# The first load ahead of SyncE's register set-up in an im2col kernel

## Chip, cores, metric

One core of one Trainium2 chip. The metric is the device time of one execution in microseconds (us). All runs used for a verdict are of state "fast". Ratios are the mean time of one kernel's fast runs over that of the other's of the same rounds, so they are not quite the ratio of the medians quoted beside them.

## The reference

```python
# x: (16, 64, 32, 32) float32, kernel_size 3
for b in range(batch):
    col_idx = 0
    for i in range(h_out):              # 30
        for j in range(w_out):          # 30
            patch = x[b, :, i:i + 3, j:j + 3]
            cols[b, :, col_idx] = patch.ravel()
            col_idx += 1                # cols: (16, 576, 900)
```

4.19 MB are read and 33.18 MB are written.

## The kernel before

The partitions carry 8 planes of 32 x 32 each. Two loads bring them in (planes 0 and 1, then the other six), VectorE and ScalarE copy nine shifted windows of each plane, and four stores of two planes each write the result. When the program is otherwise complete, the first load is taken out of the body and put into the program's head, ahead of the barrier of all engines.

```python
    first = load(0, 2 * H)
    load(2 * H, CPP * H)
    # ... (cut)
    for c in range(0, CPP, 2):
        out_tile = out_pool.tile([P, 2, KK, HO, WO], x.dtype, name="out_tile")
        # ... six copies a plane pair on VectorE, three on ScalarE (cut)
        nc.sync.dma_start(
            out=out_v[:, c : c + 2].rearrange("p c n -> p (c n)"),
            in_=out_tile.rearrange("p c kk i j -> p (c kk i j)"),
        )
    return first
# ... (cut)
    tc.compile()
    blocks = tc.nc.main_func.blocks
    load = first.ins
    home = next(b for b in blocks if any(i.name == load.name for i in b.instructions))
    home.instructions = [i for i in home.instructions if i.name != load.name]
    head = list(blocks[0].instructions)
    at = next(
        k
        for k, i in enumerate(head)
        if i.engine == load.engine and type(i).__name__ == "InstDrain"
    )
    head.insert(at, load)
    blocks[0].instructions = head
```

## Time and profile before

| | before |
|---|---|
| time, 3 runs at first | 91.21 us (91.16 to 91.29) |
| span of the profile | 89.6 us |
| DMA queue, share of 16 engines' span | 97.2% |
| first load: issue, first packet, landed | 0.00, 1.01, 4.91 us |
| second load: issue, landed | 0.79, 12.19 us |
| last store landed | 88.81 us |

The span runs from the first instruction of the program to the last. What lies outside of it (1.8 us in the profiled execution) the profile doesn't show. The landing times are those at which a transfer's semaphore reaches its full count. The lines themselves are in the prediction.

### The profile page before, as it was taken

What the parts mean: (1) busy time and instruction counts of PE and PEld (TensorE: products, weight loads), DVE (VectorE), ACT (ScalarE), POOL (GpSimd) and SP (SyncE); (2) the same over time, 40 slices, a digit from 0 to 9 for tenths busy, and PEclk for the clock granted to TensorE, in tenths of its full rate; (3) what the DMA queues carried; (4) which work ended last, traced back from release to release, by engine and by line L of the source; (5) the groups of instructions that cost most, each with busy time, mean ns of one, the idle gap of its engine ahead of it and who ended that gap; (6) DMA issues with size and microseconds to landing.
All of it is one profiled execution on the core that took longest, in us unless ns stands there. A gap on an engine that the chain in (4) does not pass through costs nothing.

```text
span 89.6 us, 96 instructions
## 1 busy us (share of the span) xinstructions
DVE 22.6 (25%) x24; ACT 23.8 (27%) x13; POOL 0.2 (0%) x4
## 2 busy tenths in 40 slices
DVE  0079759900000099500000399100000000000000
ACT  5079759900000099500000399100000000000000
POOL 0000000000000000000000000000000000000000
DMA  5989899999999999947999999999999982999990
GB/s 128 505 384 494 362 463 463 463 463 463 463 463 463 463 463 463 434 174 318 463 463 463 463 463 463 463 463 463 463 463 463 463 347 116 463 463 463 463 463 0
DMA packets 864, 37.37 MB, mean 417 GB/s; under 512 B 96, under 2 KB 96, under 8 KB 96
## 3 DMA queue, kind: packets, MB, share of 16 engines
q1 hardware_dynamic: 864, 37.37, 97.2%
HBM read 4.19 MB, written 33.18 MB: 417 GB/s over the span
## 4 chain that ended last, share of the span: by engine, by line
DMA 49%; DVE 12%; DVEq 1%; issue 0%; SPq 0%
DMA out_dram<-out_tile 36%; DMA in_tile<-in_x_dram 13%; DVE out_tile L57 8%; DVE out_tile L61 2%; DVE out_tile L65 1%; DVEq L89 1%; DVEq L57 0%; SPq L71 0%
## 5 line engine op out<-in xcount | busy, mean ns | idle before, releaser
L55 ACT COPY out_tile<-in_tile 128x2700 f32<-128x2700 f32 x8 | 19.2, 2443 | 31.7 <-DMA out_dram<-out_tile 27.1
L57 DVE COPY out_tile<-in_tile 128x1800 f32<-128x1800 f32 x16 | 16.8, 1092 | 33.7 <-DMA out_dram<-out_tile 27.1
L61 DVE COPY out_tile<-in_tile 128x1800 f32<-128x1800 f32 x4 | 4.4, 1090 | 0.0
L68 ACT COPY out_tile<-in_tile 128x900 f32<-128x900 f32 x4 | 3.8, 938 | 0.0
L65 DVE COPY out_tile<-in_tile 128x900 f32<-128x900 f32 x4 | 2.5, 620 | 0.0
L55 ACT ACT_TABLE_LOAD x1 | 1.3, 1283 | 0.8 <-PEq L118 0.8
L118 POOL MEMSET const-bfloat16-1.0<- 128x1 bf16 x1 | 0.1, 101 | 0.0
L118 POOL MEMSET const-uint8-127<- 128x1 uint8 x1 | 0.1, 101 | 0.0
L118 POOL MEMSET const-float32-0.0<- 128x1 f32 x1 | 0.1, 98 | 0.2 <-issue 0.2
L118 POOL MEMSET const-float32-1.0<- 128x1 f32 x1 | 0.1, 98 | 0.0
## 6 DMA issues: line engine op xcount, KB each, us to landing
out_dram<-out_tile SPq DMA_DIRECT2D x4, 8100.0 KB, 32.4
in_tile<-in_x_dram SPq DMA_DIRECT2D x1, 3072.0 KB, 11.4
in_tile<-in_x_dram SPq DMA_DIRECT2D x1, 1024.0 KB, 4.9
```

The source lines that it names most:

```text
L55: nc.scalar.copy(out=o[:, K : 2 * K], in_=planes(c + s, 1, 0, K, 1))
L57: nc.vector.tensor_copy(out=o[:, ki * K : ki * K + 2], in_=planes(c + s, ki, 0, 2, 1))
L61: nc.vector.tensor_copy(out=o[:, 2:KK:6], in_=planes(c + s, 0, 2, 2, 2 * W))
L65: nc.vector.tensor_copy(out=o[:, 2], in_=in_tile[:, c + s, 0:HO, 2 : 2 + WO])
L68: nc.scalar.copy(out=o[:, 8], in_=in_tile[:, c + s, 2 : 2 + HO, 2 : 2 + WO])
L89: tc.compile()
L118: nc = _bacc.Bacc("TRN2", target_bir_lowering=False, num_devices=1)
```

## The change

Its intent: the six set-up instructions of SyncE (five register moves and one load of a base address) stand ahead of the first load. Putting the load ahead of them should start the transfers earlier.

```diff
     head = list(blocks[0].instructions)
-    at = next(
-        k
-        for k, i in enumerate(head)
-        if i.engine == load.engine and type(i).__name__ == "InstDrain"
-    )
+    at = next(k for k, i in enumerate(head) if i.engine == load.engine)
     head.insert(at, load)
```

## The prediction

> **What bounds the kernel now.** I read the page first (utilisation, the forty slices, the queues), then the chain that ended last, then the instructions of the first microsecond, then the packets one by one.
>
> ```profile
> span 89.6 us, 96 instructions
> DVE 22.6 (25%) x24; ACT 23.8 (27%) x13; POOL 0.2 (0%) x4
> DMA  5989899999999999947999999999999982999990
> q1 hardware_dynamic: 864, 37.37, 97.2%
> ```
>
> The compute engines are busy a quarter of the span. The one DMA queue is busy 97.2% of 16 engines' span: 0.972 x 89.6 = 87.1 us per DMA engine. The transfers are the bound. (The dips in the DMA row are packets of 2.4 us counted in the slice where they begin, not pauses: where I sampled the packets every 0.5 us, all 16 engines had one in flight from 1.5 to 88.0 us but for one moment, near 11.5 us.)
>
> ```profile
> 0.79 11.40 DMA in_tile<-in_x_dram
> 17.95 32.59 DMA out_dram<-out_tile
> 50.56 0.05 DVEq L57
> 55.77 0.54 DVE out_tile L65
> ```
>
> The chain of waits (start, length, what) follows the last *compute* instruction, which is not what ends the program: it stops at 56.3 us, while the last store lands at 88.81 us. So I set the end from packets instead. The first data packet of the first load starts at 1.01 us, the last packet of the last store ends at 88.33 us, 87.32 us in all. One engine carries 8 packets of the first load (mean 378 ns, 3.02 us), 8 of the second (912 ns, 7.30 us) and 32 of the stores (2397 ns, 76.72 us): 87.04 us. A mean engine has 0.28 us without a packet, nearly all of it between the second load's last packet (ends 11.24 to 11.83) and the first store's first (starts 11.54 to 11.84). The engine that ends last has none there: its load ends at 11.834 and its store starts at 11.836. The end is therefore the first packet's start plus uninterrupted transfer.
>
> ```profile
> start us, us, engine line op out<-in xcount [idle before <-releaser]
> 0.00 1.12 SPq L35 DMA_DIRECT2D in_tile<-in_x_dram  x2
> 0.23 0.10 POOL L118 MEMSET const-float32-0.0<- 128x1 f32 x1 [0.23 <-issue]
> 0.78 1.28 ACT L55 ACT_TABLE_LOAD   x1 [0.78 <-PEq L118]
> ```
>
> The timeline of the first microsecond: time zero of the span *is* the first load's issue. It is already ahead of the barrier of all engines. What stands before it on SyncE, five register moves and one load of a base address, is not among the 96 instructions shown; the page leaves register instructions out. The second load is issued at 0.79, right behind the barrier.
>
> ```profile
> L118 SPq DRAIN  x1: 132/132/132, 0.4 to 0.4; - x1
> L118 SPq EVENT_SEMAPHORE  x1: 17/17/17, 0.7 to 0.7; - x1
> L118 POOLq DRAIN  x1: 179/179/179, 0.3 to 0.3; - x1
> L35 SPq DMA_DIRECT2D in_tile<-in_x_dram x2: 332/357/382, 0.0 to 0.8; - x2
> DMA to landing us min/median/max: 4.9/8.2/11.4
> ```
>
> The instructions of the barrier's line and the loads' line (ns min/median/max, first and last start). SyncE's drain (0.43 to 0.56) is the last of the four arrivals; GpSimd's own drain ended at 0.48. So SyncE holds the barrier by about 0.1 us.
>
> [...]
>
> **The change part by part.** *Removed from ahead of the first load:* the set-up, call its time d. No row holds it, so I estimate it from the neighbours. GpSimd has four such moves between the end of its semaphore instruction (158 ns) and its first memset (231 ns): 73 / 4 = at most 18 ns each. SyncE's own short instructions take 7 (drain) to 17 ns (semaphore). So five moves are 5 x 10 to 18 = 50 to 90 ns[...]. Sum d = 70 to 140 ns, middle 100.[...]
>
> *Moved behind the load:* the same d, now between the first issue and SyncE's drain. In absolute time the drain cannot begin later than before, since the same instructions run in another order. It may end earlier: the 132 ns for which it lasts look like waiting for the issue to finish (SyncE's later drains take 7 ns), and now the moves lie in that time. If so the barrier opens up to 564 - 479 = 85 ns earlier and the second load goes up to that much earlier. That is worth nothing: its first packet starts at 3.97 us, and issued at 0.79 it could have started near 0.79 + 0.85 = 1.64 us. There are 2.3 us of slack.
>
> *Added:* nothing. Work, bytes, packets and later waits are the same.
>
> *On the path:* the first packet starts d earlier; the sixteen engines then run through both loads without a pause, so the second load also ends d earlier. The first store needs the copies of the first two planes: landing 4.91 -> copies to 10.6 -> issue 10.69 -> packets 11.54. This branch begins with the first load's landing too, so it also moves by d, and no new gap opens at 11.5. Every store follows, and the end moves by d. Sum: 91.21 - 0.10 = 91.11 us.
>
> **Where I chose.** The measured time must see d. The profiled execution took 91.39 us by the same clock that gave 91.21, against a span of 89.60: 1.79 us lie outside the span[...]. I take it to open before SyncE's set-up[...]; 85% likely. The profile's *span*, which begins at the load itself, will then not show the gain: it stays 89.6.
>
> **The rivals.**
> 1. *No gain at all.* Either the first transfer's start hangs on something tied to the launch and not to the issue, or the measured window opens at the first load. For: the first load needs 1.01 us to its first packet, 0.16 more than a store, and its first packets are slow (up to 1147 ns where the fastest take 309). Against: 35 ns of it is just the longer issue (382 against 347)[...]. Time: 91.2.
> 2. *An early issue is a colder one.* The load would be the first instruction that SyncE fetches, with registers still unset; its issue of 382 ns is already the longest of the six (332 to 347 for the others).[...] Even if it gave back d and 0.1 more: 91.3. Against: [...]nothing in the trace says that the issue waits.
> [...]
> 4. *The barrier takes the gain back*, because SyncE comes later to it. For: SyncE is the last to arrive. Against: only relative to the load, not absolutely, as shown, and the second load has 2.3 us of slack. Time: as predicted, 91.1.
>
> **Range and chances.** The middle is 91.11. Repeats of one kernel spread by 0.13 us (91.16 to 91.29). From below: d at its bound of 0.25 less scatter, 90.95. From above: no gain plus scatter, 91.26. Two per cent would be 1.8 us, more than everything that precedes the first packet (1.01 us) together with the set-up; the change has no part that could reach it. Faster by over 2%: 1%; within 2%: 98%; slower: 1%[...].
>
> **What would show it.** In the changed profile: span 89.6 within 0.15; the first load's issue still at 0.00; everything on the other engines later by d *relative to it*: GpSimd's first memset at 0.33 instead of 0.23, ScalarE's table load at 0.79 to 0.88. SyncE's first drain shorter than 132 ns. The first load lands at 4.9 and the last store at 88.8 after the first issue, as now, and the queue is busy 97%. Wrong would be: the memset still at 0.23 (then d is nil or the load didn't move); a first issue well above 382 ns or a first packet later than 1.1 us (rival 2); a landing later than 5.0 us with the memset moved by d (rival 1); a new hole in the transfers near 11.5 us; or a time under 90.9 or over 91.3.

The sum came to d = 70 to 140 ns, middle 100, and so to 91.21 - 0.10 = 91.11 us. It had two terms: 50 to 90 ns for the five moves, an estimate from the 73 ns and the 7 to 17 ns that stand there, and one for the base-address load, which was the author's assumption. The 0.25 us bound at the range's lower end was not shown. The 0.85 us used for the slack is measured: the first store of `before` is issued at 10.69 us and its first packet starts at 11.54.

## The result and the profile after

The changed kernel took 91.31 us (91.21 to 91.42, 6 runs) against 91.20 us (91.12 to 91.29, 6 runs) for the kernel before; ratio 1.0011, 95% interval 0.9998 to 1.0024. The forecast was 91.11, with a range of 90.95 to 91.26; 91.31 lies outside it.

First the page of the changed kernel:

```profile
span 89.6 us, 96 instructions
q1 hardware_dynamic: 864, 37.37, 97.2%
```

Then its timeline of the first microseconds (start us, us, engine, line, operation):

```profile
0.00 1.12 SPq L35 DMA_DIRECT2D in_tile<-in_x_dram  x2
0.23 0.10 POOL L114 MEMSET const-float32-0.0<- 128x1 f32 x1 [0.23 <-issue]
0.79 1.28 ACT L55 ACT_TABLE_LOAD   x1 [0.79 <-PEq L114]
```

The prediction named this as the test: GpSimd's first memset had to move from 0.23 to 0.33, since the load was to start earlier than everything else. It stayed at 0.23. The prediction also said what that would mean: "d is nil or the load didn't move". Next, all instructions of the barrier's line (now L114, engine, operation, count, ns min/median/max, first and last start in us), and the loads' line:

```profile
L114 POOLq EVENT_SEMAPHORE  x2: 17/17/17, 0.6 to 0.7; - x2
L114 DVEq DRAIN  x1: 10/10/10, 0.1 to 0.1; - x1
L114 ACTq DRAIN  x1: 8/8/8, 0.1 to 0.1; - x1
L114 POOLq INC_SWDGE_SEM  x1: 27/27/27, 0.1 to 0.1; - x1
...
L114 SPq DRAIN  x1: 132/132/132, 0.4 to 0.4; - x1
L114 SPq EVENT_SEMAPHORE  x1: 17/17/17, 0.7 to 0.7; - x1
```

```profile
L35 SPq DMA_DIRECT2D in_tile<-in_x_dram x2: 333/358/383, 0.0 to 0.8; - x2
DMA to landing us min/median/max: 4.9/8.1/11.4
```

In the trace's own numbers the starts of the first 0.9 us are those of before to within 2 ns: SyncE's drain at 432 after 431, the second load's issue at 792 after 791. Had six instructions moved from ahead of the load to behind it, the drain would have come later after the load by their time; behind eight moves that really run it starts at 0.9 us (`moves_behind_scratch`).

**What the program holds.** So I compared the list that the kernel's Python edits with what the traces list. SyncE's head is, in the list and in the trace (starts in ns):

```
edited list, before   move, base load, move x4, LOAD 1, drain, semaphore, branch
edited list, after    LOAD 1, move, base load, move x4, drain, semaphore, branch
trace, before         LOAD 1 at 0, drain at 431, semaphore, LOAD 2 at 791
trace, after          LOAD 1 at 0, drain at 432, semaphore, LOAD 2 at 792
```

The two traces list the same 96 instructions, engine by engine in the same order, and no register move on any engine. I also built both kernels and compared the finished programs, and found the instruction streams equal; that is my own comparison and not a run. What takes the set-up out between the edited list and the chip, no trace shows. By the traces the change is a change of the text alone, and 91.31 against 91.20 must be scatter. The experiments test that, and then the other steps of the prediction in programs in which the set-up is real.

### The profile page after: what moved, and what is told of

It is laid out like the page before. It is cut to its first block, busy times and chain, and to the rows that moved or that the text cites. A ratio compares the mean times of both kernels' runs of the same rounds, so it can differ in the third digit from the quotient of the medians.

```text
span 89.6 us, 96 instructions
## 1 busy us (share of the span) xinstructions
DVE 22.6 (25%) x24; ACT 23.8 (27%) x13; POOL 0.2 (0%) x4
## 3 DMA queue, kind: packets, MB, share of 16 engines
q1 hardware_dynamic: 864, 37.37, 97.2%
## 4 chain that ended last, share of the span: by engine, by line
DMA 49%; DVE 12%; DVEq 1%; issue 0%; SPq 0%
DMA out_dram<-out_tile 36%; DMA in_tile<-in_x_dram 13%; DVE out_tile L57 8%; DVE out_tile L61 2%; DVE out_tile L65 1%; DVEq L89 1%; DVEq L57 0%; SPq L71 0%
## 5 line engine op out<-in xcount | busy, mean ns | idle before, releaser
L114 POOL MEMSET const-uint8-127<- 128x1 uint8 x1 | 0.1, 102 | 0.0
L114 POOL MEMSET const-bfloat16-1.0<- 128x1 bf16 x1 | 0.1, 101 | 0.0
L114 POOL MEMSET const-float32-0.0<- 128x1 f32 x1 | 0.1, 98 | 0.2 <-issue 0.2
L114 POOL MEMSET const-float32-1.0<- 128x1 f32 x1 | 0.1, 98 | 0.0
## 6 DMA issues: line engine op xcount, KB each, us to landing
in_tile<-in_x_dram SPq DMA_DIRECT2D x1, 3072.0 KB, 11.4
```

What stands on the lines that cost most here:

```text
L114: nc = _bacc.Bacc("TRN2", target_bir_lowering=False, num_devices=1)
```

## The experiments

Theory: the set-up isn't in the finished program, so nothing moved. Rivals: the change costs 0.1 us after all (a colder issue); the set-up ran and its time is hidden elsewhere; the first transfer's start hangs on the launch and not on the issue. Twelve kernels ran, and all gave correct results.

### The kernel before against itself, and the changed one again

Edits: none.

> The kernel before, unchanged, once more, timed against the kernel before itself. It sets the yardstick of scatter. Theory (nothing left to move: the finished program has no register set-up, both kernels give the same instruction streams): ratio 1.000, the interval's ends within 0.003 of 1, single runs spread by 0.2 to 0.3 us. Rival (the change costs 0.1 us): the same here, since nothing is changed; if this run alone shows 0.1 us, then 0.1 us is scatter.

Measured: 91.20 us (91.13 to 91.24, 5 runs) against 91.24 (91.14 to 91.32, 9 runs); ratio 0.9996 (0.9982 to 1.0009).

> The changed kernel once more, on this chip. Theory (same instruction streams): ratio to the kernel before 1.000, not reliably different from that of the unchanged copy beside it; first microsecond of the trace as before to within 2 ns. Rival (a colder issue costs 0.1 us): ratio 1.001 again and with the interval above 1. Rival (set-up moved, its time hidden elsewhere): ratio 1.000 too, but SyncE's first drain would start later after the issue than 432 ns.

Measured on the same chip in the same rounds: 91.16 us (91.05 to 91.36, 5 runs); ratio 0.9990 (0.9976 to 1.0003). Its profiled run had SyncE's drain at 432 ns as before, though the drain lasted 142 ns instead of 132, so what follows the barrier is about 11 ns later; my "within 2 ns" failed by that much, in a kernel that is word for word the changed one.

What follows: the changed kernel came out 0.1% above the kernel before in one job and 0.1% below it in the next. Both intervals include 1, and the 0.1 us didn't come back. Over all jobs the kernel before itself ran from 91.02 to 91.39 us. My range had been built on three runs that spread by 0.13 us.

### A set-up that really runs

Six moves are written ahead of the load, and the sum of their registers gives the address of the last store, so that something reads them. With them come two moves of the usual set-up: eight in all (listed in the next pair's trace as MOVE x6 and MOVE x2).

```diff
+    regs = [nc.sync.alloc_register(f"live{k}") for k in range(6)]
+    extra = [nc.sync.reg_mov(r, 1) for r in regs]
     first = load(0, 2 * H)
...
+        at = c
+        if c == CPP - 2:
+            at = sum(nc.sync.snap(r, min_val=0, max_val=1) for r in regs)
-            out=out_v[:, c : c + 2]...
+            out=out_v[:, bass.ds(at, 2)]...
...
-    head.insert(at, load)
+    head[at:at] = [*extra, load]        # moves_before_load, at SyncE's drain
+    head[at:at] = [load, *extra]        # moves_after_load, at SyncE's first instruction
```

> Six register moves that something reads (the last store's address), plus two moves of the set-up that are thereby read, stand before the first load: a set-up that really is in the program. Nothing else early differs. Theory: the moves show in the trace, at 10 to 18 ns each as I estimated, the load starts 80 to 140 ns after the first of them, and the time is 0.1 us above the kernel with the moves behind the load. Rival (the start of the first transfer hangs on the launch, not on the issue): no difference between the two. [...]against the kernel before: 91.2 plus 0.1.

Measured: 93.11 us (93.01 to 93.39, 5 runs), ratio 1.0215 (1.0198 to 1.0231).

> The same eight moves, the load ahead of them: the tested change, in a program where it has something to move. Theory: 0.1 us less than with the moves ahead, that is 91.2, as the kernel before; SyncE's drain 80 to 140 ns later after the issue, or shorter. Rival (hangs on the launch): same time as with the moves ahead. Rival (an issue as the very first instruction is colder): an issue well over 383 ns, and no gain.

Measured: 93.74 us (93.51 to 93.93, 5 runs), ratio 1.0273 (1.0256 to 1.0289).

Both missed by far. In both, the last store, whose address is now only known at run time, waits until the third has landed: in the first of the two it was issued at 70.0 us instead of 56.4, and SyncE waited at the stores' line twice for a store to land (31.7 us in all). That is a fault of my experiment. But against each other they say two things that I had not expected: the moves take far longer than I had thought (457 ns for eight), and the kernel with the load *first* is the slower one.

### The same without the fault

The six registers now give the address of a copy of 512 bytes into an unused tile, issued behind the third store; no store waits for it.

```diff
+    scratch = in_pool.tile([1, 128], x.dtype, name="scratch")
...
+        if c == CPP - 4:
+            at = sum(nc.sync.snap(r, min_val=0, max_val=1) for r in regs)
+            nc.sync.dma_start(out=scratch, in_=x_v[0:1, bass.ds(at, 128)])
```

> As the earlier run with the moves ahead of the load, but what reads the six moves is now a copy of 512 bytes into an unused tile, issued behind the third store, so that no store waits for another's landing (that wait cost both earlier runs about 1.5 us). Eight moves stand ahead of the load, at 57 ns each in the earlier trace, 0.46 us. Theory (the end follows the first issue one to one): 91.2 + 0.46 = 91.7, plus at most 0.1 for the small copy. Rival (the first transfer hangs on the launch): 91.2 to 91.3.

Measured: 91.58 us (91.56 to 91.74, 6 runs) against 91.22 (91.02 to 91.37, 11 runs); ratio 1.0047 (1.0033 to 1.0061), that is 0.43 us of 91.2. The view by line of this run, for the six moves, the two kept of the set-up, and the loads:

```profile
L44 SPq MOVE  x6: 29/29/29, 0.1 to 0.4; - x6
L129 SPq MOVE  x2: 34/37/40, 0.0 to 0.1; - x2
L38 SPq DMA_DIRECT2D in_tile<-in_x_dram x2: 339/369/399, 0.5 to 1.3; - x2
```

And its page:

```profile
span 89.8 us, 108 instructions
```

A move that runs *is* listed, with its line, and is counted: 108 instructions are the 96 of before, 9 moves, two register sums and the small copy. In the kernel before no line of any view has a MOVE. The eight moves start 51 to 70 ns apart and put the load's issue at 458 ns after the first of them; the time rises by 0.43 us. So here the end does follow the first issue, one to one.

> The same with the load first and the eight moves behind it: the second load is issued at about 1.13 us instead of 0.79. Theory as I predicted (2.3 us of slack for the second load, a later issue costs nothing): 91.2 to 91.3, that is 0.46 us under its partner. New theory (a second load issued while the first one's packets begin, at 1.1 us, has its packets slowed: 31 of 128 took 0.93 to 1.82 us instead of 0.91 in the earlier run, 0.63 us per engine): 91.8 to 92.0, no better than its partner, with such packets in the trace again. If the slow packets don't come back, that run's were something else.

Measured: 92.42 us (92.28 to 92.51, 4 runs), ratio 1.0133 (1.0114 to 1.0151). This is the tested change in a program where it has something to move, and it loses 0.78 us (0.0086 x 91.2) to its partner instead of gaining 0.46. Against the kernel before, whose first issue is also at 0, it loses 1.2 us (0.0133 x 91.2): that is what the late second load costs. The same view, of this run:

```profile
L44 SPq MOVE  x6: 29/29/40, 0.4 to 0.7; - x6
L125 SPq MOVE  x2: 29/29/29, 0.8 to 0.8; - x2
L125 SPq DRAIN  x1: 7/7/7, 0.9 to 0.9; - x1
L38 SPq DMA_DIRECT2D in_tile<-in_x_dram x2: 339/369/399, 0.0 to 1.1; - x2
DMA to landing us min/median/max: 4.6/8.3/12.1
```

SyncE's drain has shrunk from 132 ns to 7. Right behind an issue it takes 124 ns with the moves ahead and 132 in the kernel before, which fits a wait for the issue, as the prediction supposed. But the moves outlast that wait: the drain stands at 0.9 us, where it had ended at 0.56, so the barrier opens later and the second load goes at 1.14 us instead of 0.79. Its landing then takes 12.1 us instead of 11.4. The table of stretches shows where (start:end, length, busy time of VectorE, ScalarE and GpSimd with instructions, clock, DMA share, GB/s of the packets that begin in the stretch), first of the kernel before, then of this run:

```profile
3.00:5.00 2.00, 0.07 (x1) 0.07 (x1) 0.00 (x0) 1.00 1.09 463
5.00:7.00 2.00, 2.00 (x3) 2.00 (x1) 0.00 (x0) 1.00 1.20 516
7.00:9.00 2.00, 2.00 (x4) 2.00 (x2) 0.00 (x0) 1.00 0.94 406
```

```profile
3.00:5.00 2.00, 0.36 (x1) 0.36 (x1) 0.00 (x0) 1.00 1.19 467
5.00:7.00 2.00, 2.00 (x3) 2.00 (x2) 0.00 (x0) 1.00 0.80 283
7.00:9.00 2.00, 2.00 (x3) 2.00 (x2) 0.00 (x0) 1.00 1.03 430
```

From 5 to 7 us the rate is 283 GB/s where it was 516. Packet by packet: before, all 128 packets of the second load take 912 ns; here 31 take over 930 ns (up to 1667), and 17 of these, which begin between 4.2 and 6.4 us, hold most of the excess. All long packets together make 545 ns more per DMA engine, as a mean. The earlier run with the moves behind the load also has 31 long packets, 630 ns per engine.

Long packets are only part of it. Before, all 16 engines go from the first load's last packet to the second load's first without a pause (at most 7 ns). Here the first load is through at 4.27 us on all engines, and six of the 16 then have no packet until 4.50 to 4.97 us. The mean engine hides what decides: the second load has landed when its last engine is through, at 13.21 us instead of 12.19, and the span is 90.65 us instead of 89.60, 1.05 us more, where the long packets make 545 ns on the mean engine.

### Delay by another means

Empty drains of SyncE need no live register and no copy. They stand ahead of the first load, or behind it.

```diff
+    extra = [nc.sync.drain() for _ in range(20)]
     first = load(0, 2 * H)
...
+    head[at:at] = [*extra, load]        # or [load, *extra]
```

> Twenty empty drains of SyncE (7 ns each, some 50 ns apart) ahead of the first load; loads keep their distance of 0.79 us. About 1.0 us of delay. Theory (one to one): 92.2. Rival (the first transfer hangs on the launch): 91.2 to 91.4. The second load's packets stay at 912 ns, since the distance of the two issues is as before.

Measured: 92.16 us (92.03 to 92.34, 5 runs), ratio 1.0113 (1.0095 to 1.0131), so 1.03 us. The load's issue begins 1.041 us after the first drain, and every packet of the second load takes 912 ns. One to one again, with twice the dose; the rival that the first transfer's start hangs on the launch falls.

> The same twenty drains behind the first load: the first issue is at 0, the second at about 1.7 to 1.9 us, its packets are wanted at 3.97 us. Theory of slack as I predicted: 91.2. New theory (an issue later than the first packets slows the second load's packets): 91.7 or more, with packets well over 912 ns. If it is the issue at just the moment of the first packets that matters, 91.2 here and slow only with the moves.

Measured: 92.26 us as the median of 6 runs, but they spread from 91.57 to 93.78; ratio of the fast runs 1.0094 (1.0045 to 1.0144). Two runs (93.08, 93.78) count as slow by the rule that a run over 1.5% above the fastest is set aside; since this kernel scatters of itself, that label says little. The profiled run is the fastest one and has 5 long packets, 55 ns per engine. What follows: a second issue at 1.84 us costs from 0.35 us upwards, and not the same each time. Half of the runs lie below the 91.7 us that the new theory had as its least, so it is met in part only.

> Six empty drains behind the first load in place of the eight moves: the second load's issue at about 1.10 us, no live register, no small copy. Theory (the later issue alone does it): packets of the second load stretched, 91.8 to 92.5. Rival (it needs the moves): 91.2.

Measured: 92.16 us (91.61 to 92.81, 6 runs) against 91.31 (91.17 to 91.39, 11 runs); ratio 1.0094 (1.0061 to 1.0127). The second issue is at 1.105 us, and 31 packets are long again, 395 ns per engine; four engines have no packet from 4.31 us, when the first load is through, until 4.51 to 4.85. The later issue alone does it; moves and registers aren't needed.

> Seventy drains behind the first load: second issue at about 4.4 us, after the first load's last packet (3.9 to 4.6). Its packets begin near 5.3 instead of 4.0, a hole of 1.2 us in the transfers: 92.4 from that alone. If the stretch of the packets comes from an issue while the first load's packets flow, there is none here and the time is 92.3 to 92.5; if any late issue stretches them, 93 or more.

Measured: 93.66 us (93.40 to 93.78, 5 runs), ratio 1.0253 (1.0239 to 1.0267). The second issue is at 4.41 us, just after the first load's last packet has ended (4.39 us). With the hole in the transfers reckoned at 1.2 us, 92.4 was due; on top of it the *first* packet of each of the 16 engines took 1.30 to 1.85 us instead of 0.91, the other packets of the load 912 ns. So this late issue cost time with no packets of the first load under way.

### Both loads first

```diff
-    load(2 * H, CPP * H)
+    second = load(2 * H, CPP * H)
...
+    head[at:at] = [load, second.ins]    # both_loads_first
+    head[at:at] = [load, second.ins, *extra]    # both_loads_then_moves, with the eight moves
```

> As the run with the eight moves behind the first load (92.4), but with the second load also ahead of them: order first load, second load, moves. Theory (the 0.8 us that it lost came from the later issue of the second load, 1.14 instead of 0.79 us): the second issue at about 0.45, all packets of the second load 912 ns, time 91.1 to 91.3, 0.4 us under the run with the moves ahead of the load. Rival (the loss comes from the moves running while the first load is under way, or from the registers): 92.4 again.

Measured: 91.25 us (91.15 to 91.31, 5 runs) against 91.31; ratio 0.9996 (0.9984 to 1.0009). The view by line and the landings of this run:

```profile
L44 SPq MOVE  x6: 29/29/40, 0.9 to 1.2; - x6
L38 SPq DMA_DIRECT2D in_tile<-in_x_dram x2: 399/409/419, 0.0 to 0.5; - x2
DMA to landing us min/median/max: 4.7/8.1/11.5
```

All packets of the second load are back at 912 ns (one took 913), with the same moves and the same small copy. So both halves hold in these programs: getting the load ahead of a set-up that runs is worth its whole time (1.0047 to 0.9996, 0.46 us), but only if the second load goes ahead of it too (1.0133 if not). (Each ratio is against the kernel before in its own job.) The barrier isn't what costs: it opens late here too, and ScalarE's table load behind it starts at 1.61 us instead of 0.78.

> The kernel before with the second load also ahead of the barrier, right behind the first: second issue at about 0.43 instead of 0.79. If an issue before the first packets (1.01 us) is harmless and its exact moment doesn't matter: 91.2, packets at 912 ns. If earlier is better still: below 91.1, which would beat both kernels.

Measured: 91.18 us (91.16 to 91.40, 5 runs) against 91.31; ratio 0.9997 (0.9984 to 1.0009), the second issue at 0.432 us, one packet of 965 ns. No gain that can be told from scatter: no version here beats the kernel before.

## Why the prediction was wrong

**The step that failed** is the first: "What stands before it on SyncE, five register moves and one load of a base address, is not among the 96 instructions shown; the page leaves register instructions out." The page doesn't leave them out: with nine moves, two register sums and a small copy more it counts 108 instructions, not 96. They were not shown because they were not there. I had taken them from the list that the kernel's Python edits, and not from the finished program. So the term "removed from ahead of the first load", d = 70 to 140 ns, was 0, and with it the whole gain. Shown by: the same 96 instructions in both traces, no MOVE among them; a memset still at 0.23 us; and MOVE lines in those runs that have moves.

**The estimate of d** rested on "GpSimd has four such moves between the end of its semaphore instruction (158 ns) and its first memset (231 ns)". The trace lists nothing between the two, and nothing on ScalarE ahead of its drain at 128 ns; what fills the 73 ns no run here shows. A real move on SyncE measures 29 to 40 ns and 51 to 70 ns from start to start, where I had 10 to 18 for all of it.

**The rivals.** "No gain at all" was right in its time and wrong in both its reasons: the first transfer doesn't hang on the launch (1.04 us of delay gave 1.03), and the measured window does contain what precedes the load, by the same runs. The colder issue falls as well, though not by 383 ns after 382, since the load was SyncE's first instruction in both programs. It falls by the runs in which it comes first or doesn't: 399 ns behind eight moves and 399 ahead of them, 383 behind twenty drains and 383 ahead of them.

**The range** of 90.95 to 91.26 was too narrow above. Its upper end was "no gain plus scatter" from three runs; eleven runs of one kernel in one job spread over 0.35 us.

**What held.** The bound (DMA 97.2%, span 89.6), the end following the first issue, the drain's 132 ns read as a wait for the issue (7 ns behind eight moves), and 98% for a time within 2%. The span and the 98% say nothing for my mechanism: they hold for a change that does nothing. The end following the first issue was shown by the later runs alone. One reading was off without harm: of the 0.28 us in which a mean engine has no packet, only 0.15 lie between the second load and the first store, not "nearly all"; the rest is that the engines don't start and end together.

**What would have failed next.** "The second load has 2.3 us of slack" was wrong in a place where it did no harm, since the second load didn't move either. Issued at 1.10 or 1.14 us instead of 0.79 it costs 0.9 to 1.2 us, while by my count it could have waited until 3.97 - 0.85 = 3.1 us for free. Seen: at 0.43, 0.45 and 0.79 (and 0.81 after the first issue) the packets keep 912 ns but for one or two in some runs (at most 1002); at 1.10 us and later they don't. Where between 0.81 and 1.10 us it turns, and why late packets stretch, was not shown. It isn't any late issue: in the kernel before, each of the four stores is issued while earlier packets are under way, and none of their 512 packets takes over 2.44 us (2.40 as a mean).

## What to carry to other kernels

Before an instruction's time is predicted, make sure that it is in the finished program: the profile here listed every move that ran (nine among 108 instructions) and none among the 96 of both kernels. When the gain at stake is 0.1%, measure the scatter of one kernel against itself first. And when something is put between the issues of two transfers, don't read slack from when the later one's packets are due; here the second load had to be issued soon after the first one, and 0.3 us more between them cost 0.9 to 1.2. Nor should such a loss be read from a mean over the DMA engines: here the long packets made 545 ns in the mean, and the span grew by 1.05 us.
